# A hybrid attention kernel: the rotary stage's matmuls in program order, and the decay rows of the delta-rule heads loaded a head earlier

## The chip, the cores and the metric

The kernel runs on one NeuronCore of a Trainium2 chip. The metric is the device time of one execution in microseconds; less is better. The median of three runs before the change is 3652.25 us (3650.98 to 3652.95).

## The reference

Two layers, each with two branches over the same 1,056 tokens (1,024 of a prompt, 32 of a running stream) and 1,024 channels. The input is normalized and projected by one wide matrix. Branch A is a gated delta rule with a causal convolution, 8 heads; branch B is differential attention with rotary positions, 8 heads. Cut to what matters here:

```python
h, gate = ada_norm(x, c, p['norm_w'], p['w_ada'], p['b_ada'])
u_a, z_a, b_a, a_a, q_b, k_b, v_b, z_b, g_a, g_b = split_cols(h @ p['w_in'])
u_a, conv_new = causal_conv_silu(u_a, conv_buf, p['conv_w'])
beta = jax.nn.sigmoid(b_a)
g = -jnp.exp(p['a_log']) * jax.nn.softplus(a_a + p['dt_bias'])
o_a, ssm_new = gated_delta_rule(q_a, k_a, v_a, g, beta, ssm0)
...
# gated_delta_rule, by blocks: G is the running sum of g, the "decay rows"
dec_incl = jnp.exp(jnp.where(incl, G[..., :, None] - G[..., None, :], -jnp.inf))
a_mat = jnp.eye(L) + bc[..., :, None] * kk * dec_strict
sol = lax.linalg.triangular_solve(a_mat, rhs, left_side=True, lower=True, unit_diagonal=True)
...
q_b = rope(q_b ..., pos); k_b = rope(k_b ..., pos)   # x1*cos - x2*sin, x1*sin + x2*cos
o_b = diff_attn_core(q_b, k_b, v_b, lam, mask)
merged = sigmoid(g_a) * (o_a @ w_proj_a) + sigmoid(g_b) * (o_b @ w_proj_b)
x = x + gate * (merged @ w_out)
return x, k_b, v_b, ssm_new, conv_new
```

The rotated keys `k_b` are an output, one row for each token.

## The kernel before

For precision each matmul operand is split into a high and a low part (`whi`, `wlo` for weights, two tiles for activations) and three products are added, so a weight is copied by ScalarE (`whi`), the rest is subtracted on VectorE or GpSimd (`wlo`), and 24 matmuls fill one output tile of 128 channels by 384 tokens (288 in the last of three groups). A planner orders each engine's instructions when the kernel is built: of those that are ready by its own estimate of time it takes the earliest in program order. `urgent()` moves instructions ahead in that order. Inside `manual_schedule` TensorE's instructions keep program order instead.

Stages of a layer, in order:

1. **Branch A's heads** (`gdn1`, L544, called from L1377 on; up to about 551 us in layer 0, 1950 to 2317 us in layer 1). For each head three projections of 24 matmuls by 3 groups go through PSUM tiles `pd` (two buffers, L83) to `u`, are convolved, and are turned to token rows (`ptt`, `kt`, `vt`). The head's decay rows `Gb` (576 KB, each row broadcast to 128 partitions) are loaded by SyncE's queue after the projections (L548), into one buffer. ScalarE makes `eg` of them (L586), VectorE multiplies it with `q`, masks `Gb`, and nine chunks follow, each with three small matmuls (`ptk`), `E`, and a record `rec` (two buffers) that is stored to HBM.
2. **Rotary projections** (`rope_pair`, L785): eight calls, four for queries and four for keys. Call 0 stands in the code of stage 1, calls 1 to 7 from L1415 on. For each of three groups two PSUM tiles (`pr`) are filled, VectorE multiplies each by cos and by sin (`rt`), GpSimd combines (`ro`), the result is stored; for keys TensorE turns it to token rows at once (`ptk`), ScalarE copies it (`ko`), and that is stored too.
3. **Inverse** (`invert`, L645), interleaved in the code with stage 2: 64 steps over the triangular blocks of all heads, each step `itmp` and `X` on VectorE for columns up to `CUT` = 26 and on GpSimd for the rest, then a copy to `ub` (L667), the stores, and 31 small steps for the 32 stream tokens in the same two buffers. The code takes it up 16 steps at a time, between two calls of stage 2.
4. **Merge and scan** (L1447): TensorE in program order; other projections (`vals`, `zproj`, `proj`) fill the gaps by a budget of `pad(ns)`. First 42 us of it (`P_INV`), then `merge_inverse` loads the inverse's blocks (`mxy`, `mu`, `mP`) and multiplies them (`ptm`).
5. **Attention**, also in program order with the same fill, then the closing projections.

## Time and profile before

| | |
|---|---|
| median of three runs | 3652.25 us |
| the profiled execution | 3643.02 us, span 3641.2 us |
| TensorE busy with matmuls | 3366.1 us, 92% of the span |
| VectorE, ScalarE, GpSimd busy | 2170.1, 1509.9, 1343.5 us |
| mean granted TensorE clock | 0.97 of 2.4 GHz |
| DMA | 526.66 MB, mean 145 GB/s |

Times in the rows are microseconds from the start of the span. In a timeline row the first two numbers are start and duration, and the bracket at the end says how long the engine sat idle before and on whom. A tile's name `out<-in` tells which instruction it is; lines such as L54 or L69 are helpers through which all instructions of a kind go. Granted clock 1.00 is 2.4 GHz and 0.50 is 1.2 GHz; a number between is a mixture of both in that stretch.

### The profile page before, as it was taken

How to read it: one execution, taken by the hardware profiler on the slowest of the kernel's cores; microseconds unless marked ns; L12 is line 12 of the kernel's file. 1: busy time of each engine (PE TensorE's matmuls, PEld its weight loads, DVE VectorE, ACT ScalarE, POOL GpSimd, SP SyncE). 2: the span in 40 equal slices, each digit the busy share in tenths (PEclk: the TensorE clock that was granted, in tenths of full speed). 3: DMA queues.
4: the chain of work that ended last, by engine and by line, in shares of the span. 5: the costliest groups of instructions: out<-in, count | busy, mean ns of one | idle time of the engine just before them, and what ended most of it. 6: DMA issues, size and time to landing. Idle time of an engine off the chain costs nothing.

```text
span 3641.2 us, 58240 instructions
## 1 busy us (share of the span) xinstructions
PE 3366.1 (92%) x20880; PEld 3142.2 (86%) x20880; DVE 2170.1 (60%) x3682; ACT 1509.9 (41%) x4182; POOL 1343.5 (37%) x1131
## 2 busy tenths in 40 slices
PE   8988897899999999899999999879999999999999
PEld 6888897878988998899888989878898899888897
DVE  5676758851436566764447776687143456676554
ACT  4565552123544444543244656311254344444321
POOL 2355548811124343423012223693011443343310
PEclk9999999899999999999999999999999999999999
DMA  5445544356744444546433444424676434454644
GB/s 180 112 147 143 150 121 129 85 161 195 230 144 121 139 129 136 172 142 189 135 130 95 120 120 112 139 71 139 186 228 181 132 117 134 148 149 144 181 150 150
DMA packets 618985, 526.66 MB, mean 145 GB/s; under 512 B 107028, under 2 KB 567448, under 8 KB 618312
## 3 DMA queue, kind: packets, MB, share of 16 engines
q1 hardware_dynamic: 618696, 522.94, 49.0%
q8 instruction: 165, 2.70, 0.3%
q14 instruction: 124, 1.02, 0.1%
HBM read 342.49 MB, written 180.31 MB: 144 GB/s over the span
## 4 chain that ended last, share of the span: by engine, by line
PE 37%; DMA 7%; DVE 5%; POOL 4%; issue 3%; ACT 2%; SPq 0%; DVEq 0%; POOLq 0%; ACTq 0%
PE pd L72 20%; PE ptok L72 7%; DMA Gb<-grow 2%; PE pav L72 2%; PE psc L72 2%; DMA eo<-ob 2%; PE pr L72 1%; PE pts L72 1%; POOL X L54 1%; PE pta L76 1%; POOL itmp L54 1%; PE po L72 1%; POOL ro L54 1%; POOL wlo L54 1%; DMA kraw<-kscr 1%
## 5 line engine op out<-in xcount | busy, mean ns | idle before, releaser
L72 PE MATMUL pd<-h,whi 128*128 128x384 f32 (+1 forms) x2688 | 702.7, 337 | 16.2 <-ACT u L69 13.1
L72 PE MATMUL pd<-mg,whi 128*128 128x384 f32 (+1 forms) x2688 | 694.9, 335 | 11.9 <-ACT u L69 11.8
L54 POOL TENSOR_TENSOR wlo<-wraw,whi 128x512 fp32r<-128x512 f32 (+1 forms) x220 | 429.8, 1963 | 584.8 <-ACT whi L69 526.2
L72 PEld LDWEIGHTS pd<-h,whi 128*128 128x128 f32 x2688 | 476.0, 193 | 24.8 <-ACT u L69 14.4
L72 PEld LDWEIGHTS pd<-mg,whi 128*128 128x128 f32 x2688 | 474.0, 192 | 19.5 <-ACT u L69 12.7
L72 PE MATMUL pd<-h,wlo 128*128 128x384 f32 (+1 forms) x1344 | 450.0, 335 | 0.0
L72 PE MATMUL pd<-mg,wlo 128*128 128x384 f32 (+1 forms) x1344 | 449.8, 335 | 0.0
L69 ACT CAST whi<-wraw 128x1024 fp32r<-128x1024 f32 (+1 forms) x304 | 259.3, 865 | 200.9 <-PE pd L72 63.2
L72 PEld LDWEIGHTS pd<-h,wlo 128*128 128x128 f32 x1344 | 259.6, 193 | 2.5 <-issue 1.2
L72 PEld LDWEIGHTS pd<-mg,wlo 128*128 128x128 f32 x1344 | 258.9, 193 | 2.8 <-issue 1.2
L72 PE MATMUL ptok<-whi,mg 128*128 128x512 f32 x768 | 241.4, 395 | 5.2 <-DVE rt L54 3.4
L66 ACT ACTIVATE e<-psc,nm 32x160 f32<-32x160 f32 (+2 forms) x144 | 101.1, 702 | 327.1 <-DVE nm L1025 185.8
L63 DVE SCALAR_TENSOR_TENSOR acc<-u,convT,acc 128x1059 f32<-128x1059 f32 x144 | 219.1, 1525 | 2.7
L72 PE MATMUL pr<-mg,whi 128*128 128x384 f32 (+1 forms) x768 | 196.6, 339 | 15.7 <-DVE rt L54 15.7
L72 PE MATMUL pr<-h,whi 128*128 128x384 f32 (+1 forms) x768 | 194.7, 339 | 13.6 <-DVE rt L54 13.6
L72 PE MATMUL pd<-ob,whi 128*128 128x384 f32 (+1 forms) x768 | 186.5, 327 | 10.2 <-ACT ob L69 8.5
L72 PE MATMUL pd<-oa,whi 128*128 128x384 f32 (+1 forms) x768 | 193.2, 330 | 0.0
L54 DVE TENSOR_TENSOR wlo<-wraw,whi 128x1024 fp32r<-128x1024 f32 x84 | 109.3, 1302 | 119.5 <-ACT whi L69 117.4
L72 PEld LDWEIGHTS ptok<-whi,mg 128*128 128x128 f32 x768 | 144.2, 189 | 37.9 <-DVE rt L54 3.6
L72 PE MATMUL psc<-k,qh 128*128 128x512 f32 (+3 forms) x416 | 142.9, 351 | 29.5 <-DVE e L63 29.3
L54 DVE TENSOR_TENSOR itmp<-ub,X 128x624 f32<-128x624 f32 (+56 forms) x188 | 152.2, 810 | 15.7 <-DMA ub<-ublks 6.2
L72 PEld LDWEIGHTS pr<-mg,whi 128*128 128x128 f32 x768 | 140.6, 199 | 20.3 <-DVE rt L54 19.6
(315 smaller groups left out, 7983.9 us busy)
## 6 DMA issues: line engine op xcount, KB each, us to landing
wraw<-in_w_in SPq DMA_DIRECT2D x160, 512.0 KB
srec<-grec SPq DMA_DIRECT2D x128, 384.0 KB
grec<-rec SPq DMA_DIRECT2D x128, 192.0 KB
z<-zo SPq DMA_DIRECT2D x96, 192.0 KB
wraw<-in_w_ada SPq DMA_DIRECT2D x64, 256.0 KB
qraw<-qscr SPq DMA_DIRECT2D x128, 128.0 KB
egt<-z SPq DMA_DIRECT2D x64, 192.0 KB
eo<-ob SPq DMA_DIRECT2D x60, 192.0 KB
```

Of the source, the lines that this page charges most:

```text
L54: (eng or s.nc.vector).tensor_tensor(out, a, b, op=op)
L63: s.nc.vector.scalar_tensor_tensor(out, a, sc, b, op0=op0, op1=op1)
L66: s.nc.scalar.activation(out, a, func, **kw)
L69: s.nc.scalar.copy(out, a)
L72: s.nc.tensor.matmul(out, lhsT, rhs, start=start, stop=stop)
L76: s.nc.tensor.transpose(out, a, s.ident[0:n, 0:n])
```

## The change

- `gdn1`: `Gb` is loaded by a function `decay(hd)` on ScalarE's DMA queue. Head 0 loads its own after its projections as before; each head then issues the load of the next head's rows. `Gb` has two buffers, `rec` three.
- `rope_pair`: cos, sin and the combination are `urgent()`, as is the store of the result. The key rows of a group are turned after the next group's matmuls (`turn_keys`, `key_rows`). The results `ro` have a pool of four buffers of their own in the loop of calls 1 to 7.
- In that loop TensorE is in program order, `pd` has four PSUM buffers instead of two, and the inverse advances by 4 steps after each group instead of by 16 between two calls.
- The PSUM pool `pd` is opened for each stage instead of once; two small tiles of the modulation code move to the `ev` pool.

```diff
@@ -80,7 +80,7 @@
         tc, nc = s.tc, s.nc
         P = lambda name, bufs=1, **kw: st.enter_context(tc.tile_pool(name=name, bufs=bufs, **kw))
         s.dp = P("scratch", space=DRAM)
-        s.pd = P("pd", 2, space=PSUM)
+        s.turned = None
         s.cpool = P("const")
         s.gp = s.cpool
         s.wp = P("w", 2)
@@ -244,7 +244,7 @@
         for kk in range(0, KT, 2):
             x = s.wload(w, kk, 2, c0, 256, pool=s.mp, eng=s.nc.gpsimd)
             s.accumulate2(pm[:, 0:256], [(s.cst[:, kk + k, :], x[k][i]) for k in range(2) for i in range(2)], kk == 0, kk == KT - 2)
-        row = s.mp.tile([4, 256], F32, tag="mrow", name="mrow")
+        row = s.ev.tile([128, 384], F32, tag="ev", name="mrow")[0:4, 0:256]
         s.cp(row, pm[0:4, 0:256])
         for j in range(2):
             s.tr(pm[:, 256 + j * 4:260 + j * 4], row[:, j * 128:(j + 1) * 128])
@@ -264,7 +264,7 @@
             s.ts(gt[:, j], s.md[l][:, 16:24, j], 0.5)
         ps = s.pm.tile([128, 512], F32, tag="pm", name="psm")
         s.tr(ps[0:16, 0:128], gt.rearrange("p a b -> p (a b)"))
-        gr = s.mp.tile([16, 128], F32, tag="gr", name="gr")
+        gr = s.ev.tile([128, 384], F32, tag="ev", name="gr")[0:16, 0:128]
         s.cp(gr, ps[0:16, 0:128])
         s.st.dma_start(out=s.grd[l], in_=gr)
 
@@ -543,10 +543,18 @@
 
     def gdn1(s, l, pool, h, hd, cv, gates=None):
         nc = s.nc
+
+        def decay(hd):
+
+            Gb = pool.tile([128, NC, 128], F32, tag="Gb", name="Gb")
+            nc.scalar.dma_start(out=Gb, in_=s.grow[l][:, hd, :].partition_broadcast(128))
+            return Gb
+
         kq, v = s.conv_head(l, pool, h, hd, cv, gates)
         k, q = kq[:, 0], kq[:, 1]
-        Gb = pool.tile([128, NC, 128], F32, tag="Gb", name="Gb")
-        s.ld.dma_start(out=Gb, in_=s.grow[l][:, hd, :].partition_broadcast(128))
+
+        Gb = s.decay if hd else decay(0)
+        s.decay = decay(hd + 1) if hd < H - 1 else None
 
         kt = pool.tile([128, NC, 128], F32, tag="kt", name="kt")
         vt = pool.tile([128, NC, 128], F32, tag="vt", name="vt")
@@ -662,7 +670,7 @@
                         s.tt(t, ub[:, j, j + 1:B].unsqueeze(2).to_broadcast([nb, m, c1 - c0]),
                              X[:, j:j + 1, c0:c1].to_broadcast([nb, m, c1 - c0]), OP.mult, eng=eng)
                         s.tt(X[:, j + 1:B, c0:c1], X[:, j + 1:B, c0:c1], t, OP.subtract, eng=eng)
-                if j % 8 == 7:
+                if j % 4 == 3:
                     yield
             nc.vector.tensor_copy(ub.rearrange("p a b -> p b a"), X)
             s.st.dma_start(out=pdst, in_=ub)
@@ -782,7 +790,7 @@
                 last(c, 0 if (i - 5) % H == 0 else 4)
 
 
-    def rope_pair(s, l, pool, wpools, h, c_base, pr, dst, tabs, out):
+    def rope_pair(s, l, pool, wpools, h, c_base, pr, dst, tabs, out, step=None):
 
         nc = s.nc
         W = []
@@ -806,7 +814,7 @@
             W.append((hi, lo))
         cos, sin = tabs
         for g, (t0, n) in enumerate(GROUPS):
-            o = [s.ev.tile([128, 384], F32, tag="ev", name=f"ro{e}") for e in range(2)]
+            o = [s.rop.tile([128, 384], F32, tag="ev", name=f"ro{e}") for e in range(2)]
             sl = slice(t0, t0 + n)
             tm = []
             for e in range(2):
@@ -815,24 +823,38 @@
                                          for k in range(KT) for a, b in ((0, 0), (0, 1), (1, 0))])
                 for x, tab in enumerate((cos, sin)):
                     tmp = s.ev.tile([128, 384], F32, tag="ev", name=f"rt{e}{x}")
-                    s.tt(tmp[:, :n], ps[:, :n], tab[:, sl], OP.mult)
+                    with s.urgent():
+                        s.tt(tmp[:, :n], ps[:, :n], tab[:, sl], OP.mult)
                     tm.append(tmp)
-            s.tt(o[0][:, :n], tm[0][:, :n], tm[3][:, :n], OP.subtract, eng=nc.gpsimd)
-            s.tt(o[1][:, :n], tm[1][:, :n], tm[2][:, :n], OP.add, eng=nc.gpsimd)
+            with s.urgent():
+                s.tt(o[0][:, :n], tm[0][:, :n], tm[3][:, :n], OP.subtract, eng=nc.gpsimd)
+                s.tt(o[1][:, :n], tm[1][:, :n], tm[2][:, :n], OP.add, eng=nc.gpsimd)
+                for e in range(2):
+                    s.st.dma_start(out=dst[pr * 4:pr * 4 + 4, e * 32:e * 32 + 32, sl], in_=o[e][:, :n])
+
+            s.turn_keys()
+            if out:
+                s.turned = lambda o=o, g=g, t0=t0: s.key_rows(l, pool, pr, o, g, t0)
+            if step:
+                step()
+        yield
+
+    def turn_keys(s):
+        f, s.turned = s.turned, None
+        if f:
+            f()
+
+    def key_rows(s, l, pool, pr, o, g, t0):
+
+        for c in range(g * 3, min(g * 3 + 3, NC)):
+            m, c0 = csize(c), c * 128 - t0
+            pt = s.pt.tile([128, 512], F32, tag="pt", name="ptk")
             for e in range(2):
-                s.st.dma_start(out=dst[pr * 4:pr * 4 + 4, e * 32:e * 32 + 32, sl], in_=o[e][:, :n])
-            if not out:
-                continue
-            for c in range(g * 3, min(g * 3 + 3, NC)):
-                m, c0 = csize(c), c * 128 - t0
-                pt = s.pt.tile([128, 512], F32, tag="pt", name="ptk")
-                for e in range(2):
-                    s.tr(pt[:m, e * 128:(e + 1) * 128], o[e][:, c0:c0 + m])
-                ko = pool.tile([128, 4, 2, 32], F32, tag="ko", name="ko")
-                s.cp(ko[:m], pt[:m, 0:256].rearrange("p (e g d) -> p g e d", e=2, g=4))
-                d = s.io["k_prompt"][l, 0, pr * 2:pr * 2 + 2, c * 128:c * 128 + 128, :] if c < 8 else s.io["k_sample"][l, 0, pr * 2:pr * 2 + 2]
-                s.st.dma_start(out=d.rearrange("h t f -> t h f"), in_=ko[:m].rearrange("p (h m) e d -> p h (m e d)", h=2))
-        yield
+                s.tr(pt[:m, e * 128:(e + 1) * 128], o[e][:, c0:c0 + m])
+            ko = pool.tile([128, 4, 2, 32], F32, tag="ko", name="ko")
+            s.cp(ko[:m], pt[:m, 0:256].rearrange("p (e g d) -> p g e d", e=2, g=4))
+            d = s.io["k_prompt"][l, 0, pr * 2:pr * 2 + 2, c * 128:c * 128 + 128, :] if c < 8 else s.io["k_sample"][l, 0, pr * 2:pr * 2 + 2]
+            s.st.dma_start(out=d.rearrange("h t f -> t h f"), in_=ko[:m].rearrange("p (h m) e d -> p h (m e d)", h=2))
 
     def v_proj(s, l, pool, h):
 
@@ -1347,8 +1369,7 @@
 
             h = acts("h")
             with ExitStack() as st:
-                s.pb = psum(st, "pb0", 2)
-                s.pt = psum(st, "pt0", 1)
+                s.pd, s.pb, s.pt = psum(st, "pd0", 2), psum(st, "pb0", 2), psum(st, "pt0", 1)
                 tmp = pool(st, "start", 1)
                 s.start(h, tmp, pool(st, "startw", 8), pool(st, "startx", 3))
             for l in range(L):
@@ -1359,18 +1380,20 @@
                 nc.vector.memset(s.s0, 1.0)
                 nc.vector.memset(s.sso, 1.0)
                 tabst = ExitStack()
+                s.rop = s.ev
                 tabs = []
 
-                def rope(n, wpools, out):
+                def rope(n, wpools, out, step=None):
                     pr, qk = divmod(n, 2)
-                    return s.rope_pair(l, out, wpools, h, (C_QB, C_KB)[qk], pr, (s.qscr, s.kscr)[qk][l], tabs, qk == 1)
+                    return s.rope_pair(l, out, wpools, h, (C_QB, C_KB)[qk], pr, (s.qscr, s.kscr)[qk][l], tabs, qk == 1, step)
 
 
                 with ExitStack() as st:
-                    s.pt = psum(st, f"pta{l}", 3)
+                    s.pd, s.pt = psum(st, f"pda{l}", 2), psum(st, f"pta{l}", 3)
                     g1 = pool(st, f"a1{l}", 1)
                     g2 = s.Multi(pool(st, f"a3{l}", 2), g1, ("acc", "kq"))
-                    g2 = s.Multi(pool(st, f"a2{l}", 2), g2, ("u", "E", "rec", "us", "sk", "r", "ir", "rc", "ks", "sq", "kqh"))
+                    g2 = s.Multi(pool(st, f"a2{l}", 2), g2, ("u", "E", "us", "sk", "r", "ir", "rc", "ks", "sq", "kqh", "Gb"))
+                    g2.m["rec"] = pool(st, f"a4{l}", 3)
                     s.tmp4 = g1
                     mods, sm = [(i, part, c) for i, part in ((1, 0), (1, 1), (0, 2), (1, 2)) for c in range(4)] if l == 0 else [], ExitStack()
                     cv = g1.tile([128, 2, 3, 24], F32, name="cv")
@@ -1406,17 +1429,17 @@
                 v2.m["vo"] = pool(vst, f"v3{l}", 2)
                 vals = s.v_proj(l, v2, h)
                 with ExitStack() as st:
-                    s.pt = psum(st, f"ptb{l}", 2)
+                    st.enter_context(tc.manual_schedule(engines={mybir.EngineType.PE}))
+                    s.pd, s.pt = psum(st, f"pdb{l}", 4), psum(st, f"ptb{l}", 2)
+                    s.rop = pool(st, f"ro{l}", 4)
                     b1 = pool(st, f"b1{l}", 1)
                     b2 = s.Multi(pool(st, f"b2{l}", 2), b1, ("ko",))
                     s.sample_stat(v2, h)
                     inv = s.invert(l, b1)
 
-                    for n in range(8):
-                        if n:
-                            drain(rope(n, [s.wp if n % 2 else v2] * 2, b2))
-                        for _ in range(2):
-                            next(inv, None)
+                    for n in range(1, 8):
+                        drain(rope(n, [s.wp if n % 2 else v2] * 2, b2, lambda: next(inv, None)))
+                    s.turn_keys()
                     drain(inv)
                 tabst.close()
 
@@ -1441,6 +1464,8 @@
 
                 s.fill = fillers()
                 s.left = 24 * T / 2.4 * 40 + 2 * (8 * 24 + 16) * 512 / 2.4
+                pdc = ExitStack()
+                s.pd = psum(pdc, f"pdc{l}", 2)
                 order = ExitStack()
                 order.enter_context(tc.manual_schedule(engines={mybir.EngineType.PE}))
 
@@ -1475,8 +1500,10 @@
                     drain(s.attn(l, c2))
                     s.pad(1e9)
                 order.close()
+                pdc.close()
 
                 with ExitStack() as te:
+                    s.pd = psum(te, f"pde{l}", 2)
                     xs = pool(te, f"xs{l}", 2)
                     with ExitStack() as tb:
                         p12 = pool(tb, f"ob{l}")
```

## Rows read from the trace of the kernel before

**Rows 1.** Windows view: stretch, length, busy (count) of PE, PEld, DVE, ACT, POOL; PEclk.

```profile
375.00:450.00 75.00, 65.55 (x427) 63.22 (x426) 57.84 (x83) 45.40 (x139) 43.49 (x44) 0.95 0.52 150
...
600.00:675.00 75.00, 59.15 (x323) 56.22 (x321) 65.56 (x64) 9.62 (x19) 73.36 (x52) 0.91 0.26 72
...
3075.00:3150.00 75.00, 73.32 (x481) 70.26 (x481) 47.04 (x94) 36.76 (x98) 31.20 (x22) 1.00 0.49 148
```

**Rows 2.** Waits, layer 0's branch A: waiter and releaser, total us, times, longest.

```profile
ACT eg L66 <- DMA Gb<-grow: 63.6, 8, 8.8
...
ACT rec L66 <- DMA grec<-rec: 39.0, 27, 5.9
```

**Rows 3.** Timeline of SP's queue, ACT, DVE and PE, one head of layer 1.

```profile
2079.59 0.42 SPq L549 DMA_DIRECT2D Gb<-grow  x1
...
2089.35 1.16 ACT L66 ACTIVATE eg<-Gb 128x1152 f32<-128x1152 f32 x1 [6.09 <-DMA Gb<-grow]
...
2090.55 1.33 DVE L54 TENSOR_TENSOR eg<-kq,eg 128x1024 f32<-128x1024 f32 x2 [5.71 <-ACT eg L66]
...
2091.04 0.66 PE L76 MATMUL ptt<-ident,v 128*128 128x128 f32 x4 [2.75 <-ACT vt L69]
```

**Rows 4.** Timeline of PE: the first and the last of 17 such gaps.

```profile
180.97 0.53 PE L72 MATMUL pd<-h,whi 128*128 128x288 f32 x2 [3.85 <-ACT u L69]
...
2280.43 0.85 PE L72 MATMUL pr<-mg,whi 128*128 128x288 f32 x2 [1.97 <-DVE rt L54]
```

**Rows 5.** Windows view, the 10 us after one of those gaps.

```profile
2177.00:2187.00 10.00, 10.00 (x50) 9.97 (x50) 7.08 (x7) 5.89 (x24) 1.89 (x4) 0.77 0.34 98
```

**Rows 6.** Windows view, the rotary stages of both layers.

```profile
551.00:770.00 219.00, 181.27 (x1010) 170.16 (x1009) 178.01 (x213) 35.13 (x69) 164.16 (x139) 0.93 0.41 118
2317.00:2525.00 208.00, 172.38 (x970) 162.86 (x970) 175.30 (x209) 31.23 (x62) 161.06 (x136) 0.93 0.39 115
```

**Rows 7.** Waits of PE, rotary stages: two rows of layer 0, one of layer 1.

```profile
PE ptk L76 <- POOL ro L54: 21.7, 7, 6.8
PE pr L72 <- DVE rt L54: 8.1, 7, 1.9
...
PE ptk L76 <- POOL ro L54: 15.0, 7, 6.6
```

**Rows 8.** Timeline of PE: matmuls of one rotary tile, three per half microsecond.

```profile
541.29 0.51 PE L72 MATMUL pr<-h,whi 128*128 128x384 f32 x2
...
541.82 0.51 PE L72 MATMUL pr<-h,whi 128*128 128x384 f32 x2
```

**Rows 9.** Timelines: end of layer 0's inverse to the first merge; layer 1's two ends.

```profile
744.51 3.81 DVE L667 COPY ub<-X 128x4096 f32<-128x4096 f32 x1
...
763.02 2.55 SPq L650 DMA_DIRECT2D ub<-ublks  x2
...
793.30 1.11 DVE L667 COPY ub<-X 8x1024 f32<-8x1024 f32 x1
...
794.83 0.64 SPq L680 DMA_DIRECT2D mxy<-xblk  x1
...
798.64 1.11 PE L72 MATMUL ptm<-mxy,mu 64*64 64x64 f32 x16 [0.73 <-DMA mu<-u]
...
2508.77 3.72 DVE L667 COPY ub<-X 128x4096 f32<-128x4096 f32 x1
...
2560.73 1.14 PE L72 MATMUL ptm<-mxy,mu 64*64 64x64 f32 x16
```

**Rows 10.** Timeline of POOL: one inverse operation twice, in the same shape.

```profile
623.24 0.84 POOL L54 TENSOR_TENSOR X<-X,itmp 128x352 f32<-128x352 f32 x1
...
662.33 1.68 POOL L54 TENSOR_TENSOR X<-X,itmp 128x352 f32<-128x352 f32 x1
```

**Rows 11.** Timelines of POOL and PE: call 1's first combination, head 7's last chunk.

```profile
539.00 1.99 POOL L54 TENSOR_TENSOR ro<-rt,rt 128x384 f32<-128x384 f32 x2 [3.35 <-DVE rt L54]
...
547.27 0.20 PE L72 MATMUL ptk<-kql,kqh 128*32 128x64 f32 x1
```

## Prediction

> **What bounds the kernel now.** I read the windows view first, over the whole span in stretches of 75 us. It shows two kinds of stretch [rows 1]. From the merge stage to the end TensorE is busy nearly without a break (73.3 of 75 us at a granted clock of 1.00, that is 2.4 GHz): it is the bound there, and what it does there it does after the change too. In branch A's heads it is busy 65.6 of 75 us and in the rotary stage 59.2, both at a lower clock, although neither VectorE nor ScalarE is full in the first. So the change can win only in these two stages, and the question in each is who keeps TensorE waiting and what it would wait for next.
>
> For branch A I went from the view of waits to the timelines. ScalarE's costliest wait in layer 0's heads is for the decay rows, 63.6 us in eight waits; the wait of the records for a free buffer comes to 39.0 us in 27 short ones [rows 2]. One head shows how the first reaches TensorE [rows 3]: SyncE issues the load at 2079.6, ScalarE sits until 2089.35 for it, VectorE behind ScalarE, and the turned values (`vt`) that ScalarE would have copied meanwhile hold a PSUM buffer, so TensorE's next transpose comes 2.75 us late. I then went through TensorE's timeline of both layers and kept the gaps that end within a few microseconds of such an end, in heads 1 to 7 alone (head 0's load isn't moved ahead). There are 17 of them, nine in layer 0 and eight in layer 1; the first is 3.85 us and the last 1.97 [rows 4]; they add up to 39.3 + 29.3 = 68.6 us. No other gap of TensorE in these stages is over 1.6 us, head 0's aside. After a long gap the clock is low for a while: 0.77 in the 10 us after the gap that ends at 2176.7 [rows 5], which is 2.3 us of work lost.
>
> For the rotary stage the windows view of its two stretches [rows 6] leaves TensorE idle 219.0 - 181.3 = 37.7 us and 208.0 - 172.4 = 35.6 us, at a mean clock of 0.93. Who it waits for [rows 7]: mostly the key rows' transposes for GpSimd's combination (21.7 us in layer 0, at most 6.8 at a time), then a PSUM buffer that VectorE has not emptied (8.1 us). But VectorE (178.0 us) and GpSimd (164.2 us) are nearly full in the same stretch, with the inverse, and the merge stage cannot begin before the inverse is done [rows 9].
>
> **The change, part by part.** *Decay rows a head ahead.* The same 16 loads of 576 KB move from SyncE's queue to ScalarE's. One costs its queue 0.42 us [rows 3], so ScalarE gives 7 us in all, hidden, since it is busy 45 of 75 us [rows 1]. The load is then issued a head before its use (eight heads fill some 476 us of layer 0), against 10 us from issue to use now. In ScalarE's queue it stands behind the last use of its buffer, which is ScalarE's own, so it blocks nothing. Of the 68.6 us I count all as removed, and for the clock 12 gaps of the 14 heads at 1.5 us, a little under the row at 2.3, which is 18. The sum is 86.6. Lower bound: half of it, 43, if ScalarE's next wait is close behind. I take 80%, -70, because TensorE is then the fullest engine by far and VectorE and ScalarE have 17 and 30 us of 75 to spare [rows 1]. Head 0's load now waits on ScalarE for the store of the same rows; between nothing and a further 6 us, the length of a decay wait [rows 3], I take 1 for each layer, +2.
>
> *Third record buffer.* The 39.0 us are ScalarE's, covered by the next head's projections on TensorE: nothing. In head 7, where only rotary matmuls cover it, it shortens the chain; counted with the junction below.
>
> *The junction.* `pd` is closed after branch A and four new PSUM buffers are opened over its banks and over those of `pt`. Two are free at once; the third tile of call 1 must wait for head 7's last chunks. Before, call 1 ran between them: its first combination started at 539.0, so its third tile was already running, and head 7's last chunk matmul came at 547.3 [rows 11]. Price from 0 to 8.3 us plus the few by which the matmul leads; half, 4 in each layer, +8, since head 7 loses its own decay wait and much of its record waits.
>
> *Four PSUM buffers, keys a group later, program order.* Three matmuls start every 0.53 us [rows 8], so a tile of 24 takes 4.2 us and the next group's two tiles 8.5. That covers GpSimd's longest delay of 6.8 us [rows 7], and two more tiles in PSUM cover VectorE's. The `wlo` of the next call costs GpSimd the same as before. TensorE itself then loses up to 37.7 and 35.6 us of gaps and some 10 of clock in each layer (0.07 of 219 is 15, part of it while idle): 93 us in all, if it is the bound. Program order takes the fill of value projections out of the stage; it is done afterwards and costs nothing twice.
>
> *What is late next: the inverse.* The merge needs it, and its work on VectorE and GpSimd stays the same. From the start of the big copy to the first merge matmul are 54.1 us in layer 0 and 52.0 in layer 1 [rows 9]. In there the reload for the stream tokens is issued at 763.0, 14.7 us after the copy's end at 748.3, in a queue that holds the last rotary call's stores; those now come earlier, so I take 12 off, leaving a store and its landing. The 30 us from this reload to the last small copy are a chain and stay, and so do the loads behind it. The copy itself moves by VectorE's idle time at most: 41 us in the stretch [rows 6], part of it after the copy. I take 5 us. So the merge starts 17 us earlier in each layer, -34, and TensorE, which arrives some 48 us earlier, waits about 30 us for it. Bounds: nothing and -93.
>
> Why only 5: the same GpSimd operation takes 0.84 us at one time and 1.68 at another [rows 10], so VectorE and GpSimd stretch each other, and their busy time holds waiting that no order of theirs removes. The Trainium skill says that outright: under "SBUF — State Buffer", section "SBUF: two separate sides", VectorE with two operands in SBUF and GpSimd lock each other out of one port pair for a whole instruction. The row's factor of two agrees. By that rule the copy would not move at all, and the sum below would be 10 us smaller.
>
> *The rest* (the two small tiles in `ev`, pools opened for each stage) is counted at nothing: layer 0's modulation is covered by the heads' matmuls, and from 1 to 2 us if not.
>
> **Sum.** -70 + 2 + 8 - 34 = -94 us, from the profiled execution's 3643.0 to 3549. That execution is 9.2 us below the median of the three runs, 3652.25, so I add 9 and predict **3558 us**.
>
> **The rivals.** *TensorE is the bound of the rotary stage.* Then the merge isn't held by the inverse, the 93 us count whole: -70 + 10 - 93 = -153, or 3499 us. For it: some of the chain in rows 9 is queueing. Against: VectorE and GpSimd are full [rows 6]. Chance 0.20.
>
> *The inverse can't be moved.* VectorE and GpSimd hold each other up as in rows 10, and its copy ends when it did; only the shorter queue behind it gains, 24 us in both layers: -84, or 3568 us. This is the case of the page named above; the rows bear out a factor of two for some instructions, not for all. Chance 0.20.
>
> *ScalarE finds another wait.* The records' 39.0 us [rows 2], or copies that the planner puts behind something else, take half of the gaps back: -35 instead of -70, -59 in all, or 3593 us. For it: ScalarE works in strict order and 27 short waits remain possible. Against: a third buffer. Chance 0.15.
>
> *Slower: the inverse is pushed back.* Rotary work is urgent on VectorE and GpSimd and the planner puts it in front by its own estimate of when a tile is full; where TensorE is later than that, VectorE stands still before a `pr` with inverse work behind it, and TensorE in program order has no fill. The place is VectorE's queue in the rotary stage, the price 1 us for each us by which the merge starts later. With branch A at -60 net it decides from 30 us a layer on; at 45 us it gives +30, or 3682 us. For it: VectorE idled 41 us in the stretch [rows 6]. Against: 45 us is more than all of that again. Chance 0.07.
>
> *The change does nothing:* the planner's new order opens other gaps of the same size. 3652 us, chance 0.03.
>
> **How the numbers follow.** The forecast has 0.35, the rivals 0.20, 0.20, 0.15, 0.07 and 0.03. A measurement of this kernel can tell about 0.2%, 7 us, from no change. Faster by more: 0.35 + 0.20 + 0.20 + 0.15 = 0.90; within: 0.03; slower: 0.07. The range reaches from the TensorE-bound case with a little more from branch A's upper bound, 3490, to the case of half the gaps with no gain in the rotary stage's queue, 3593 + 24 = 3617, rounded to 3615.
>
> **What would show it.** Branch A: no wait of `eg` on the decay rows over 1 us in heads 1 to 7, and TensorE at 72 or more of 75 us there; if another releaser stands in the gaps, the third rival. Junction: a gap of 4 us before call 1's third tile, on a `ptk` of head 7. Rotary stage: no wait of the key transposes on `ro` above 2 us, the stage's matmuls done in about 160 us, and a gap of some 30 us before the first `ptm`, ended by `mxy` or `mu`; without that gap, the first rival; with a gap over 60 us, the slower one. The prediction is wrong if branch A keeps its gaps, or if the merge starts later, counted from branch A's end, than 248 us (798.6 - 551).

## The result, and the profile after

The changed kernel takes **3669.76 us** (median of five runs, 3666.76 to 3671.71) against 3652.25 for the kernel before: a ratio of 1.0055, 95% interval 1.0042 to 1.0068. It is 0.5% slower, where 3558 us was predicted, outside the range of 3490 to 3615. The profiled execution takes 3669.8 us, its span 3667.9.

The windows view in the three stretches of [rows 1] (stretch, length, busy of PE, PEld, DVE, ACT, POOL, clock):

```profile
375.00:450.00 75.00, 67.10 (x436) 64.72 (x435) 54.74 (x82) 45.87 (x137) 42.57 (x44) 0.93 0.52 152
600.00:675.00 75.00, 53.50 (x286) 50.93 (x285) 64.51 (x62) 8.56 (x17) 73.28 (x54) 0.82 0.26 72
3075.00:3150.00 75.00, 73.24 (x489) 70.64 (x488) 43.44 (x85) 36.77 (x97) 30.53 (x21) 1.00 0.43 125
```

The last stretch is as it was. Branch A's heads are hardly better (67.1 us busy at 0.93 is about as much work as 65.6 at 0.95), and in the rotary stage TensorE is busy 53.5 us at a clock of 0.82 where it was 59.2 at 0.91.

**Branch A.** ScalarE's waits in layer 0, as in [rows 2]:

```profile
ACT eg L66 <- DMA Gb<-grow: 56.6, 7, 9.9
ACT rec L66 <- DMA grec<-rec: 21.6, 16, 3.4
```

The record waits are nearly halved, the decay waits are not: 56.6 us in seven instead of 63.6 in eight. ScalarE's timeline around the sixth head of layer 1, and the gap of TensorE behind it:

```profile
2143.36 0.37 ACTq L550 DMA_DIRECT2D Gb<-grow  x1
...
2153.69 1.16 ACT L66 ACTIVATE eg<-Gb 128x1152 f32<-128x1152 f32 x1 [5.86 <-DMA Gb<-grow]
2154.76 0.57 ACT L69 COPY vt<-ptt 128x512 f32<-128x512 f32 x1
...
2155.38 0.66 PE L76 MATMUL ptt<-ident,kq 128*128 128x128 f32 x4 [2.54 <-ACT vt L69]
```

The load is issued a head early, as soon as its buffer is free, and the exponential of it stands a head early too: 10.3 us from issue to use, no less than in [rows 3], and the same `vt` behind it.

**The junction.** The windows view of 20 us around head 7's chunks in both layers, first after, then before, and TensorE's timeline after:

```profile
520.00:540.00 20.00, 12.46 (x67) 10.25 (x66) 8.40 (x29) 12.29 (x45) 11.04 (x12) 0.71 0.42 134
2295.00:2315.00 20.00, 11.91 (x58) 10.09 (x57) 9.16 (x29) 12.45 (x36) 9.32 (x11) 0.74 0.47 146
```

```profile
520.00:540.00 20.00, 20.00 (x133) 19.77 (x132) 11.00 (x27) 9.24 (x33) 9.37 (x10) 1.00 0.36 105
2295.00:2315.00 20.00, 20.00 (x134) 19.95 (x133) 9.76 (x26) 8.27 (x23) 9.98 (x12) 1.00 0.45 134
```

```profile
524.21 0.29 PE L72 MATMUL pr<-h,wlo 128*128 128x288 f32 x1
...
538.59 0.24 PE L72 MATMUL ptk<-kqh,kql 128*32 128x64 f32 x1
538.65 0.99 PE L72 MATMUL pr<-h,whi 128*128 128x384 f32 x2
```

Now nothing fills head 7's chain of chunks. TensorE does 12.46 x 0.71 = 8.8 us of work at full clock in 20 us. Call 0 ends at 524.5, and not even the first tile of call 1 begins before head 7's last chunk matmul at 538.59 (layer 1: 2310.80, the tile at 2310.86).

**The rotary stage.** TensorE's waits from 540 to 830 us, to set beside [rows 7] (in layer 0, 21.7 us in seven waits, at most 6.8):

```profile
PE ptk L76 <- POOL ro L54: 35.2, 12, 13.0
```

The longest one, in the timelines of TensorE, VectorE and GpSimd:

```profile
608.14 0.33 PE L72 MATMUL pr<-h,wlo 128*128 128x384 f32 x1
...
618.45 0.55 DVE L54 TENSOR_TENSOR rt<-pr,cos 128x384 f32<-128x384 f32 x1
618.92 0.54 DVE L54 TENSOR_TENSOR rt<-pr,sin 128x384 f32<-128x384 f32 x1
...
619.89 1.82 POOL L54 TENSOR_TENSOR X<-X,itmp 128x360 f32<-128x360 f32 x1
...
627.22 1.62 POOL L54 TENSOR_TENSOR X<-X,itmp 128x360 f32<-128x360 f32 x1
628.81 2.85 POOL L54 TENSOR_TENSOR ro<-rt,rt 128x384 f32<-128x384 f32 x2
...
616.46 0.34 PE L72 MATMUL pr<-h,wlo 128*128 128x384 f32 x1
629.85 0.48 PE L76 MATMUL ptk<-ident,ro 128*128 128x128 f32 x1 [13.05 <-POOL ro L54]
```

The group's second tile is full at 608.5, and VectorE, with inverse steps in its own order, begins on it only at 618.45, ten microseconds later. The products are done at 619.46. GpSimd has five inverse operations in its fixed order before the combination, from 619.89 to 628.81. The PSUM buffers of the products are free by 619.46, but in TensorE's order the transposes come before the next matmuls. So both engines are late, and of the two it is VectorE that got later: over the 21 groups of calls 1 to 7 in layer 0 it begins a group's last products 6.3 us after their tile is full (2.6 before the change), GpSimd its combination 3.8 us after them (3.7 before); in layer 1 it is 5.7 (2.8) and 4.1 (3.4).

**The inverse's end**, as in [rows 9]:

```profile
725.14 3.92 DVE L675 COPY ub<-X 128x4096 f32<-128x4096 f32 x1
...
740.48 1.29 SPq L658 DMA_DIRECT2D ub<-ublks  x2
...
785.74 0.65 SPq L688 DMA_DIRECT2D mxy<-xblk  x1
...
814.00 0.39 PE L72 MATMUL ptok<-wlo,sstat 128*128 128x512 f32 x1
814.23 0.40 PE L72 MATMUL ptok<-whi,sstat 128*128 128x512 f32 x1
814.56 1.14 PE L72 MATMUL ptm<-mxy,mu 64*64 64x64 f32 x16
```

The copy starts 19.4 us earlier than before, the reload 22.5, the merge's first load 9.1. But no wait stands before the first merge matmul, which comes 15.9 us later than before: TensorE is still in the value projections that program order has put there.

### The profile page after: what moved, and what is told of

Read it like the earlier page. It is cut to its first block, busy times and chain, and to the rows that moved or that the text cites. A ratio compares the mean times of both kernels' runs of the same rounds, so it can differ in the third digit from the quotient of the medians.

```text
span 3667.9 us, 58186 instructions
## 1 busy us (share of the span) xinstructions
PE 3375.9 (92%) x20880; PEld 3146.5 (86%) x20880; DVE 2171.1 (59%) x3682; ACT 1507.5 (41%) x4182; POOL 1356.1 (37%) x1131
## 5 line engine op out<-in xcount | busy, mean ns | idle before, releaser
L72 PEld LDWEIGHTS pd<-h,whi 128*128 128x128 f32 x2688 | 474.7, 193 | 21.9 <-ACT u L69 11.1
L63 DVE SCALAR_TENSOR_TENSOR acc<-u,convT,acc 128x1059 f32<-128x1059 f32 x144 | 210.7, 1466 | 1.8
L54 DVE TENSOR_TENSOR itmp<-ub,X 128x624 f32<-128x624 f32 (+56 forms) x188 | 160.2, 852 | 25.5 <-DMA ub<-ublks 16.6
L54 DVE TENSOR_TENSOR X<-X,itmp 128x624 f32<-128x624 f32 (+56 forms) x188 | 164.3, 874 | 4.9
```

What stands on the lines that cost most here:

```text
L54: (eng or s.nc.vector).tensor_tensor(out, a, b, op=op)
L63: s.nc.vector.scalar_tensor_tensor(out, a, sc, b, op0=op0, op1=op1)
L72: s.nc.tensor.matmul(out, lhsT, rhs, start=start, stop=stop)
```

## The experiments

Each is timed beside the kernel before (medians 3647 to 3652 us), and the ratios are to that; "rotary part" means the change without its edits to branch A, "branch A's part" the reverse.

**Branch A's part alone.** The diff's `decay`, `Gb` in two buffers, `rec` in three; rotary stage of before.

> Branch A's part alone (decay rows a head ahead, three record buffers; rotary stage as before). First theory: with two decay buffers the exponential eg of the next head hangs on nothing but its load, so the planner puts it right behind the load in ScalarE's order and ScalarE still waits for the transfer: eg's waits stay near 100 us in all (102.1 in 14 in the changed kernel), 2 to 9 us each, and the time is 3645 to 3660 us, the same as before. Second theory, branch A is mended as predicted and the rotary part eats it: no wait over 1 us and 3560 to 3600 us.

3626.64 us, ratio 0.9939 (0.9925 to 0.9954): 25 us faster, in neither range, though the first theory's waits are there. `eg` waits 104.4 us in 14 waits (115.5 in 16 before). From the first `pba` to the first `pr` nothing is won (420.6 and 354.6 us in the two layers, 418.5 and 353.3 before); from the first to the last `pr`, where head 7 lies, 12 in each layer (243.6 and 243.3; 255.8 and 255.3 before). There, in layer 0, the kernel before has one decay wait of 7.5 us, head 7's, and this run none:

```profile
ACT eg L66 <- DMA Gb<-grow: 7.5, 1, 7.5
```

In layer 1 head 7's wait, 8.1 us, is gone from there too: with the exponential a head early it now stands ahead of the first `pr`, where there are seven waits in each layer in both kernels. That the 12 us are this wait is concluded from its place; the third record buffer is ruled out below.

**The same, with the exponential tied to its head.** The bias is zero, so the values stay the same.

```diff
-        s.act(eg, Gb, AF.Exp)
+        z = pool.tile([128, 1], F32, tag="ez", name="ez")
+        s.ts(z, sq[:, 0, 8:9], 0.0)
+        s.act(eg, Gb, AF.Exp, bias=z)
```

> The same with one thing more: eg takes a bias of zero computed from its own head's squares, so it cannot be ordered before its head's transposes. First theory: no wait of eg for the decay rows over 1 us in heads 1 to 7, TensorE's 17 gaps behind them gone, and the predicted 70 us or a good part of them: 3570 to 3615 us. Second theory, ScalarE's next wait (records, squares) takes the place: eg's waits gone but the gaps there under other names, 3630 to 3655 us.

3588.09 us, 0.9827 (0.9813 to 0.9841). Timeline of ScalarE with the third head's load and exponential, then its largest wait in layer 0 and the windows view of layer 1's branch A up to the first `pr`, in this run and in the kernel before:

```profile
1961.14 0.37 ACTq L550 DMA_DIRECT2D Gb<-grow  x1
...
2023.92 1.24 ACT L66 ACTIVATE eg<-Gb,ez 128x1152 f32<-128x1152 f32 x1
```

```profile
ACT whi L69 <- DMA wraw<-in_w_ada: 40.0, 9, 9.0
```

```profile
1875.80:2185.70 309.90, 309.90 (x2051) 306.73 (x2050) 233.31 (x368) 197.89 (x617) 98.73 (x138) 1.00 0.46 120
```

```profile
1900.80:2254.10 353.30, 325.68 (x2068) 319.76 (x2069) 244.42 (x382) 201.98 (x637) 99.53 (x141) 0.96 0.40 107
```

The exponential comes 62.8 us after its load and waits for nothing; no decay wait is left. Layer 1's branch A, to the first `pr`, falls from 353.3 to 309.9 us with TensorE busy throughout at 1.00. Layer 0's falls only from 418.5 to 403.4: there ScalarE now waits for the modulation's weights, 40.0 us where it was 7.1, and seven gaps of TensorE, 24.8 us in all, end within 3.2 us of the end of such a wait. A part of layer 1's gain is lost again in the rotary stage, which did not get shorter with it: from the first `pba` to the first `psc` (the first matmul of attention) the layers gain 24.2 and 32.5 us. Of the 38.6 us between the two runs the planner's early exponential is the cause: it is the one edit.

**The third record buffer alone.**

```diff
-... ("u", "E", "rec", "us", "sk", "r", "ir", "rc", "ks", "sq", "kqh"))
+... ("u", "E", "us", "sk", "r", "ir", "rc", "ks", "sq", "kqh"))
+                    g2.m["rec"] = pool(st, f"a4{l}", 3)
```

> The kernel before with a third record buffer and nothing else (the two small modulation tiles moved to the ev pool for space). If the 25 us of branch A's part alone are head 7's shorter chain through the third buffer: 3625 to 3635 us. If they are the decay wait of head 7, which is taken away from the stretch where only rotary matmuls cover it: 3645 to 3655 us, as predicted for this buffer (nothing).

3652.00 us, 1.0000 (0.9986 to 1.0013): nothing, as predicted.

**The rotary part alone, with and without program order.**

> The rotary part alone (branch A's loads as before, everything else of the change in). First theory: program order makes TensorE sit while GpSimd is late with the keys' combinations, and the value projections no longer fill in; with the PSUM banks of the junction that is 7 to 12 us in a layer: 3662 to 3680 us. Second theory, the slower time of the changed kernel is branch A's alone: 3610 to 3650 us.

3693.68 us, 1.0123 (1.0105 to 1.0140): 42 us slower, 14 beyond the first theory's range. With branch A's part at -25 that is +17, and the whole change measured +18: the two parts add.

```diff
-                    st.enter_context(tc.manual_schedule(engines={mybir.EngineType.PE}))
```

> The rotary part alone without program order on TensorE in that stage (four PSUM buffers, keys a group later, urgent combinations, finer steps of the inverse all kept). First theory: the fill of value projections comes back into the gaps and 5 to 10 us a layer are won against the run with program order; what is left is the junction: 3648 to 3662 us. Second theory, the junction and the pushed-back inverse do it: no better than with program order, 3662 to 3680 us.

3681.12 us, 1.0083 (1.0070 to 1.0096). Order costs 12.6 us here, more than the second theory has it; 30 remain, more than the first has. The transposes wait on `ro` in layer 0 no less than with order: 40.5 us in 13 waits, at most 13.8, against 28.6 in 12, at most 12.3.

**The PSUM banks.** Two pools of two buffers are held through branch A (which uses the first alone) and the stage, which takes them in turn as a ring of four (`e5`, with order; `e11`, without); in `e9`, without order, there are only the two of before.

```diff
+                bst = ExitStack()
+                p1, p2 = psum(bst, f"pda{l}", 2), psum(bst, f"pdb{l}", 2)
...
-                    s.pd, s.pt = psum(st, f"pda{l}", 2), psum(st, f"pta{l}", 3)
+                    s.pd, s.pt = p1, psum(st, f"pta{l}", 3)
...
-                    s.pd, s.pt = psum(st, f"pdb{l}", 4), psum(st, f"ptb{l}", 2)
+                    s.pd, s.pt = s.Ring([p1, p1, p2, p2]), psum(st, f"ptb{l}", 2)
```

> The rotary part alone, with two PSUM banks kept free through branch A, so that the stage's four buffers lie over none of the banks in which head 7 still works. Junction theory: the stretch from 500 to 550 us, where TensorE was busy 35.8 of 50 us at a clock of 0.83 (44.5 at 0.97 before the change), comes back to 42 or more, in both layers, and the run is 15 to 22 us faster than the rotary part alone (3694): 3672 to 3679 us. Rival, the stage's own waits for the keys set the time and what is won at the junction is waited out behind GpSimd: within 5 us of 3694.

> The rotary part without program order (3681) and with the two permanent PSUM buffers of before in place of four laid over branch A's banks; urgency and keys a group later kept. Theory that the overlay costs at the junction (TensorE 36 of 50 us there against 44.5) and the four buffers bring nothing: 3650 to 3668 us. Rival, urgency is what costs and the buffers are even a help: 3678 to 3700 us.

> The rotary part without program order and with four PSUM buffers that lie over none of branch A's banks. With program order the free banks closed the gaps of 500 to 550 us and gave nothing. Theory that TensorE then only waited for the keys in its fixed order: without the order the gain stays, 3655 to 3670 us. Rival, GpSimd and VectorE set the stage's end in any case: 3675 to 3690 us.

With order 3699.87 us, 1.0132 (1.0112 to 1.0151); without it 3654.11, 1.0007 (0.9993 to 1.0020), with two buffers and 3649.96, 0.9997 (0.9985 to 1.0010), with four. The windows view at the junction, without order and first over branch A's banks, then beside them:

```profile
520.00:540.00 20.00, 15.52 (x97) 13.63 (x96) 8.38 (x22) 11.71 (x48) 10.31 (x9) 0.84 0.30 88
```

```profile
520.00:540.00 20.00, 20.00 (x137) 19.84 (x136) 8.07 (x25) 7.73 (x30) 10.38 (x9) 1.00 0.37 111
```

Without order the free banks give back 31 us, all that was left of the loss, and four buffers, keys a group later, urgency and finer steps then bring nothing over before. In all runs with free banks call 1's first tile begins where call 0 ends, and in those with the overlay only behind head 7's last chunk matmul. With order the junction is mended as well (20.00 of 20 us busy), and nothing comes of it. So program order costs 50 us with free banks and 12.6 with the overlay; the two losses overlap. TensorE's waits for the keys in layer 0 with free banks, with order and without:

```profile
PE ptk L76 <- POOL ro L54: 31.4, 10, 8.2
PE ptk L76 <- ACT ko L69: 15.0, 8, 8.1
```

```profile
PE ptk L76 <- POOL ro L54: 32.2, 9, 14.8
PE ptk L76 <- ACT ko L69: 4.7, 2, 3.8
```

What order adds here is not waits on GpSimd but on ScalarE's copies, some 10 us a layer (46.4 us in all against 36.9; in layer 1 45.8 against 34.6). The other 29 of the 50 us stand in no wait for the keys: from the first `pr` to the first `psc` TensorE is idle longer and at a lower clock, and no run takes that apart.

**Parts that turned out to be nothing**: the inverse in 16 steps between calls, as before (with order), and no urgency on `rt` and `ro` (without).

> The rotary part alone with the inverse emitted as before, 16 steps between two calls instead of 4 after each group. Theory that the finer steps push rotary work and inverse into each other: 8 to 20 us faster than 3694. Rival, the order on VectorE and GpSimd is set by urgency and readiness whatever the order of emission: within 5 us of 3694.

> The rotary part without program order and without the urgency of the rotary products and combinations (four buffers, keys a group later kept). Theory that urgent rotary work is put in front of inverse steps in a fixed order that the chip doesn't keep, so that GpSimd is held up and the keys come later: 3650 to 3668 us. Rival, the junction: 3675 to 3690 us.

3694.16 us (3693.68 with the finer steps) and 3679.88 (3681.12 with urgency). Both rivals hold.

**Work taken from GpSimd.** In `rope_pair`, with order:

```diff
-                s.tt(lo[...], rv[:, :, :, e, :], hv.bitcast(F32), OP.subtract, eng=nc.gpsimd)
+                s.tt(lo[...], rv[:, :, :, e, :], hv.bitcast(F32), OP.subtract, eng=nc.vector)
```

> The rotary part alone, with the weights' low halves (wlo) of the rotary calls made by VectorE instead of GpSimd: 24 operations, some 40 us of GpSimd's work, leave it in each layer's stage. Theory that GpSimd is the pacer of the stage, TensorE waiting for its combinations: 10 to 20 us a layer faster than 3694, 3655 to 3675 us, and the key transposes' waits on ro fall from 28.6 us to under 15. Rival, the two engines hold each other up and VectorE, 65 to 73 of 75 us busy, takes over as the pacer: 3685 to 3705 us.

3677.18 us, 1.0065 (1.0041 to 1.0088): 16.5 faster in all, less than forecast. TensorE's waits on `ro` fall from 28.6 to 17.4 us in layer 0, those on `ko` rise from 12.3 to 24.9. GpSimd is one pacer, not the only one.

**The keys two groups later**, with order and free banks, six `ro` buffers; then six `ko` buffers on top.

```diff
-        f, s.turned = s.turned, None
-        if f:
-            f()
+        while s.turned and len(s.turned) >= (1 if last else 2):
+            s.turned.pop(0)()
```

> The rotary part with program order and free PSUM banks (3700), the keys turned two groups later instead of one, with six buffers for them. Theory that program order costs its 50 us because TensorE stands before the key transposes, which are late by more than the one group of lead: the waits of the transposes on ro and ko (31.4 and 15.0 us) fall by more than half and the time to 3655 to 3680 us. Rival, GpSimd and the fill that is left over for after the stage set the time: the waits move to other places, within 8 us of 3700.

> The rotary part with program order, free banks, keys two groups later (3666), and six buffers for the copied keys instead of two. In the run before TensorE's waits for GpSimd fell from 31.4 to 3.9 us in layer 0, but those for ScalarE's copy of the keys rose from 15.0 to 41.2, and ScalarE waited 60.5 us there for the keys' stores. Theory that this store is the next thing late: the waits on ko under 8 us a layer and 3635 to 3655 us. Rival, GpSimd and VectorE set the stage's length and the waits come out elsewhere: 3660 to 3675 us.

3666.46 us, 1.0047 (1.0029 to 1.0065), and 3670.19, 1.0053 (1.0038 to 1.0067). TensorE's waits in layer 0, in the first and in the second run:

```profile
PE ptk L76 <- ACT ko L69: 41.2, 13, 11.6
PE ptk L76 <- POOL ro L54: 3.9, 3, 1.6
```

```profile
PE ptk L76 <- ACT ko L69: 41.4, 10, 17.4
PE ptk L76 <- POOL ro L54: 5.6, 5, 1.5
```

The deeper lead, with its two more `ro` buffers, gives 33 us back and all but ends the waits on GpSimd, but half of my theory fails: the waits come back on ScalarE's copies, nearly as long. As the two sums are 45.1 us where they were 46.4 (layer 1: 45.3 and 45.8), the 33 us are not these waits, and where they come from is not shown. That the keys' stores hold these fails too: with six buffers ScalarE no longer waits for a store, and the copies are as late. ScalarE's timeline there:

```profile
639.53 1.06 ACT L66 ACTIVATE wraw<-wraw 128x1024 f32<-128x1024 f32 x1 [21.79 <-POOL wlo L54]
...
645.58 1.06 ACT L66 ACTIVATE wraw<-wraw 128x1024 f32<-128x1024 f32 x1 [3.82 <-DMA wraw<-in_w_in]
646.54 0.63 ACT L69 COPY ko<-ptk 128x256 f32<-128x256 f32 x2
```

The copy stands behind the scaling of the next weights, which waits 21.8 us for a buffer that GpSimd's `wlo` frees. The wait is GpSimd's again, by way of ScalarE's queue. The other two long waits of layer 0, 10.8 and 10.7 us, end in the same way, behind weights whose load was issued when a `wlo` had ended (577.6 and 707.0); the three make up 38.9 of the 41.4 us.

**Sums.** `e16` is the changed kernel with the tied exponential; `e14` takes order out as well and frees the banks; `e15` adds `wlo` on VectorE to that; `e18` keeps order, with the tie, free banks, keys two groups later and six `ko` buffers; `e12` is branch A's part with the tie, before's rotary stage and `wlo` on VectorE.

> The changed kernel with one edit, eg tied to its own head's squares. Theory that the hoisted exponential is all that kept branch A's gain away: 3670 less some 38 (3627 less 3588), 3625 to 3640 us. Rival, the stage with program order eats it, because TensorE only comes earlier to keys that are late: over 3650 us.

> The whole change with its three faults taken out: eg tied to its own head, free PSUM banks for the stage's four buffers, no program order there. If the parts add up: branch A's 63 us and nothing from the rotary part, 3582 to 3594 us. If the rotary part of the change helps once branch A is short: under 3578 us.

> The same with the rotary calls' wlo made by VectorE: with before's rotary stage that was worth 8 us (3580 against 3588). If the parts add up: 3572 to 3588 us; if urgent work and wlo crowd VectorE: over 3590 us.

> The whole change with program order kept and four things mended: the tied exponential, free banks, keys two groups later, six buffers for the copied keys. If e17's theory holds and the parts add up with branch A's 63 us: 3570 to 3595 us, level with branch A's part alone (3588). If program order still costs: over 3600 us.

> The rotary stage of before, branch A's part with the tied exponential (3588), and the rotary calls' wlo made by VectorE. If GpSimd paces the stage of before too, 5 to 10 us a layer more: 3568 to 3580 us. If TensorE's order and fill already cover it there, or VectorE takes over: 3583 to 3600 us.

| | us | ratio to before |
|---|---|---|
| `e16` | 3636.03 | 0.9958 (0.9943 to 0.9974) |
| `e14` | 3598.95 | 0.9870 (0.9850 to 0.9890) |
| `e15` | 3595.31 | 0.9847 (0.9827 to 0.9867) |
| `e18` | 3633.89 | 0.9956 (0.9940 to 0.9971) |
| `e12` | **3580.13** | 0.9807 (0.9787 to 0.9828) |

The tie is worth 34 us in the changed kernel too, as forecast. With order the whole stays near 3635, with or without the other mends: free banks and the deeper lead, worth 23 us in the rotary part alone (`e3` to `e17`), are worth 2 here. Nor do the parts add without order: `e14` is 11 us behind branch A's part with the tie (3588.09), although the rotary part cost nothing by itself (`e11`), and `e14`, `e15` and `e18` all miss the times that adding up gave. The best leaves the rotary stage as it was but for `wlo`, 71 us under the kernel before (3651.35 beside it).

## Why the prediction was wrong

The forecast was -94 us and the change measured +17.5. Branch A's part, forecast at -68, measured -25 alone; the rotary part, forecast at -26, measured +42. So some 43 of the 111 us are branch A's and 68 the rotary part's.

**Branch A, -70: the step that failed is "of the 68.6 us I count all as removed".** I moved the load and left its first user where it was. The user hung on nothing but the load, so the planner moved it too, and ScalarE waits in order for the transfer as before: 102.1 us in 14 waits, where there were 115.5 in 16. What was won is 12 us a layer where head 7 lies. With the user tied the step measured -63, close to the 70. In layer 1 it is 43.4 us to the first `pr` and 32.5 to the first `psc`, beside my 29.3 of gaps and half of the 18 for the clock (38 in all). In layer 0 it is 15.1 and 24.2, beside 48, since there my third rival, ScalarE finding another wait, came true with the modulation's weights instead of the records.

**The third record buffer, nothing: right** (3652.00 alone). **Head 0, +2: not told apart from the rest.** In the run of branch A's part alone its exponential comes 10.6 and 10.0 us after the load's issue, 9.9 and 9.5 before; the branch A stretches are 2.1 and 1.3 us longer, with seven decay waits in each as before.

**Junction, +8: right place, and the step that failed is "Two are free at once".** None of call 1's tiles began before head 7's last chunk matmul, so I priced the wait of one tile where all of call 1 waited: nothing fills head 7's whole chain, and the clock is lower with the gaps. It measured 31 us without program order, 15 a layer instead of 4. Why not even two buffers were free is not shown.

**"That covers GpSimd's longest delay of 6.8 us": failed.** The longest wait is 13.0. The 6.8 was what was left to see where other work stood in TensorE's order; it wasn't GpSimd's delay. That one was up to 9.5 us in layer 0 and 11.1 in layer 1 before the change. The first of them, in VectorE's and GpSimd's timelines of before:

```profile
623.42 0.46 DVE L54 TENSOR_TENSOR rt<-pr,sin 128x288 f32<-128x288 f32 x1
...
633.37 2.46 POOL L54 TENSOR_TENSOR ro<-rt,rt 128x288 f32<-128x288 f32 x2
```

Nor do "two more tiles in PSUM cover VectorE's": they ended TensorE's waits for a buffer (8.1 us to 1.8 in layer 0), but VectorE then came to the tiles later, and that time is in the keys' path. Program order is not why the waits on `ro` grew, since they are as long without it (`e4`); but it did cost 12.6 to 50 us, where I had written that the fill it takes away "costs nothing twice".

**Merge, -34: failed.** Counted from head 7's last chunk matmul (547.3 and 2313.7 us before, 538.6 and 2310.8 after), the copy came 10.7 and 9.2 us earlier in the two layers, against 5. From its end to the reload it took 11.4 and 12.0 us where it had been 14.7 and 12.6, so the 12 for the shorter queue were 3.3 and 0.7. But the inverse was no bound of the merge's start: TensorE was busy 47.4 of the 50 us from 750 to 800 before the change, with value projections:

```profile
750.00:800.00 50.00, 47.43 (x219) 37.81 (x219) 27.01 (x71) 9.44 (x17) 3.60 (x4) 1.00 0.52 158
```

I forecast a gap of 30 us before the first `ptm`; before the change there was one of 0.73, after it none. From the last chunk matmul to the first `ptm` it took 251 and 247 us before and 276 in both layers after: the sign that I had named for being wrong. What counted was TensorE's idle time and clock in the stage, and these got worse: from the first `pr` to the first `psc` the layers take 608.6 and 608.5 us, 601.9 and 598.2 before.

**The rivals.** "TensorE is the bound" had the right bound and the wrong sign, since it took the gaps as gone. "The inverse can't be moved" falls with the copy, some 10 us earlier in both layers. That VectorE and GpSimd stretch each other shows again in these rows of GpSimd, after the change:

```profile
633.38 1.66 POOL L54 TENSOR_TENSOR X<-X,itmp 128x357 f32<-128x357 f32 x1
635.12 0.78 POOL L54 TENSOR_TENSOR itmp<-ub,X 128x352 f32<-128x352 f32 x1
635.98 0.88 POOL L54 TENSOR_TENSOR X<-X,itmp 128x352 f32<-128x352 f32 x1
```

VectorE is at work until 634.3 and then idle for 4.4 us: nearly the same operation takes 1.66 us beside it and 0.8 without. These rows agree with the rule cited from the Trainium skill, "SBUF — State Buffer", section "SBUF: two separate sides". I take it that this also makes a fixed order on GpSimd come late, which no run isolates; it did not fix the copy's place. "Slower: the inverse is pushed back" was right that TensorE in program order has no fill and that the merge starts later, and named the wrong cause: the inverse came early, the keys late.

What stays open: why the overlay holds back even call 1's first tile, what program order costs besides the waits for the keys, and whether ScalarE's queue is all of it once the keys are led further. `e18` is 35 us behind `e14` (31 by the ratios), with 37.1 us of TensorE's waits in layer 0 on `ko` and 7.1 on `ro`; the copies stand behind `wlo`, but no run was made without that queueing.

## What to carry to other kernels

Where a planner orders an engine, a load issued earlier takes its first user along unless that user is tied to something of its own time: look for what the user waits on besides the load. The waits of an engine that has other work in its order are what is left after the filling, and no measure of how late the producer is: take that from the producer's own rows, and from those of every engine between. Putting an engine in program order takes the filling away, and its cost has to be in the sum. A stage whose buffers lie over those of the stage before it can lose the whole overlap of the two, and the price is then the length of the chain that is left alone, not of the one wait. And parts measured alone need not add up.

## What the runs showed of the hardware that was not expected

Short gaps of TensorE went with a lower granted clock. At the junction 7.5 us of idle time in 20 came with a granted clock of 0.71, so 11.2 of the 20 us at full clock were lost. Without gaps the clock stood at 1.00 (2.4 GHz) for the whole 309.9 us of layer 1's branch A in `e2`, where it had been 0.96 over 353.3 us with 27.6 idle.
